# First attention with scores from split halves, and softplus of dt on GpSimd

## The chip, the cores and the metric

The kernel runs on one core of one Trainium2 chip. The metric is the device time of one execution in microseconds (us). A program of this size is compared by the median of several executions.

## The reference, cut to what matters

The program is two blocks of a network over 256 tokens of width 1024, in fp32: an even layer, an odd layer and a further block, each a mixer with projections, attention, and a wide feed-forward. The change lies in the mixer of the even layer, the first stage of the program:

```python
proj = rms_norm(x, mix_norm) @ w_in
q, k, v, z, xbc, dt_raw = jnp.split(proj, EVEN_SPLITS, axis=-1)
q = rms_norm(q.reshape(Bsz, S, 8, 64), na_q_norm)
k = rms_norm(k.reshape(Bsz, S, 8, 64), na_k_norm)
na_out = neighbourhood_attention(q, k, v, na_rel_bias)
...
xbc = jax.nn.silu(centred_depthwise_conv(xbc, conv_w, conv_b))
...
dt = jax.nn.softplus(dt_raw.reshape(Bsz, S, 2, 16) + dt_bias)
A = -jnp.exp(A_log)
y_fwd = ssd_scan(xs, dt[:, :, 0], A[0], bm, cm)
y_bwd = jnp.flip(ssd_scan(jnp.flip(xs, 1), jnp.flip(dt[:, :, 1], 1), A[1], ...), 1)
...
return jnp.concatenate([na_out, ssd_out], axis=-1) @ w_out
```

The attention has 8 heads of 64: its scores are q k^T / 8 plus a bias, over the 256 keys, then a softmax and the values. The scan works in two chunks of 128 tokens; its decays are exponentials of running sums of `dt * A`, so nearly all of it needs dt.

## The kernel before, in words

**Number format.** A product in fp32 takes TensorE two passes. The kernel avoids that for its weights: each fp32 operand is written as a sum of a high part, rounded to the format fp32r, and a low part, the remainder, also in fp32r. A product is then three fp32r matmuls, high by high, high by low and low by high (`mm3`, L144 to L148; they are recorded at L137). For a weight, `wsplit` (L115) has ScalarE copy the loaded block into `wh` (L124) and VectorE subtract it from the block into `wl` (L126); six such pairs of buffers rotate. For activations the same is done behind a transpose.

**Order.** The program is written with generators: `gemm` yields after each block of 128 rows of a weight, `weave` and `pipeline` run several generators in turn, `defer(n, fn)` calls `fn` after n further blocks. The framework under it then schedules the instructions of each engine in an order of its own, by priorities: `tc.high_priority()` lifts what is inside, `pin` keeps an instruction in program order on its engine. So an edit can move instructions far from it. Each engine works through its own queue in order; an instruction that waits holds all behind it. PSUM has eight banks: four for accumulators, two for transposes (`tp_tile`) and two for scores and other short products (`sc_tile`).

**The even mixer up to the scan.** The projections come in the order: q (`e0`), a part of the convolution input, k (`e1`), the rest of the convolution input for the states B and C, then the columns of v and dt (`ev0`), the rest of v (`ev1`). What matters for the change:

- `done_v` (L571) writes the raw dt into `dv` (128 tokens x 64: two halves of the tokens, two directions, 16 heads).
- `softplus` (L220 to L239) computes dt from it. `nv` (L227) is -|v|, ScalarE takes the exponential (L228), `e + 2` (L229) and its reciprocal (L230) give z = e / (e + 2), and the logarithm is a polynomial in z squared (L231 to L236, seven of the steps fused as add and multiply); L237 and L238 add the positive part. All but the exponential is on VectorE, 128 x 64 each, and each step needs the one before. The tiles show as `sp_dt` in the profile. It is called under high priority (L645). The same function serves the forget gate of the last block (L1147).
- `av` (L652) is dt times A. `sums` (L659) multiplies it by triangles on TensorE (`rows`), writes the sums as high and low parts (`LH`, L666 and L667) and sends them through HBM into `RH`. `borders` (L680) makes four further sums (`cps`, L683), their exponentials and `wde` (L685, L686).
- `cb_products` (L599) makes the scan's products of C and B into a bank of `sc_tile`; VectorE takes two masked pieces, `cu` and `cl` (L608), ScalarE the third, `cbo` (L610).
- `qk_T` (L581) transposes q and k into a `tp_tile`; ScalarE copies them, times the norm's gain, into `qkT`, in fp32.
- `na_unit` (L693) is one unit of the attention: two heads by 128 queries. Its scores are two fp32 matmuls of 64 rows by 256 columns (L704). `attn_unit` (L334) adds the bias and takes the minimum on VectorE (L358), the exponential on ScalarE (L366), transposes the result (L141) and multiplies by the values. Eight units run as a pipeline, with the rest of the convolution input (`xbc`, L518 to L520) and the first half of z woven between them.
- `ssd_unit` (L761) is one unit of the scan: the decay sums (`seg`, L774) from `LH` and `RH`, the masked products times dt (`dw`, L778 and L780), minimum, exponential, two weighted copies on GpSimd (`xe`, `xD`), and the products `yp` and `op` (L807, L809). Eight units run in two halves, the first with the last quarter of the convolution, the second with the second half of z and the first products of the output projection `eo`. `gate` and `gate2` take y times z, the norm, and transpose the result for `eo` (`tp_y`, L248).

GpSimd does little before the change: norms' factors, and the scaling of q and k by them (L566).

## Time and profile before

| what | us |
|---|---|
| three runs | 989.68, 989.52, 989.49 |
| their median | 989.52 |
| the profiled execution's own time | 988.49 |
| its span on the core | 986.6 |
| TensorE busy | 968.6 |
| VectorE busy | 652.4 |
| ScalarE busy | 558.8 |
| GpSimd busy | 89.4 |

The granted TensorE clock was 0.999 of full speed over the span. In the lines of the profile, PE is TensorE, PEld its weight loads (beside the matmuls), DVE is VectorE, ACT is ScalarE, POOL is GpSimd and SP the engine that issues most DMAs. L704 is line 704 of the kernel. A line of a timeline has the start in us, the duration, the engine, the line, the operation, the tile written, the tiles read, the size and how many alike follow one another (x4); in square brackets stands what it waited for. A line of windows has a stretch A:B with its length, then for each engine the busy time and the number of instructions, then the granted clock, the busy share of the DMA engines and GB/s. A matmul in fp32 is recorded as two.

### The profile page before, as it was taken

What the parts mean: (1) busy time and instruction counts of PE and PEld (TensorE: products, weight loads), DVE (VectorE), ACT (ScalarE), POOL (GpSimd) and SP (SyncE); (2) the same over time, 40 slices, a digit from 0 to 9 for tenths busy, and PEclk for the clock granted to TensorE, in tenths of its full rate; (3) what the DMA queues carried; (4) which work ended last, traced back from release to release, by engine and by line L of the source; (5) the groups of instructions that cost most, each with busy time, mean ns of one, the idle gap of its engine ahead of it and who ended that gap; (6) DMA issues with size and microseconds to landing.
All of it is one profiled execution on the core that took longest, in us unless ns stands there. A gap on an engine that the chain in (4) does not pass through costs nothing.

```text
span 986.6 us, 13200 instructions
## 1 busy us (share of the span) xinstructions
PE 968.6 (98%) x4983; PEld 809.0 (82%) x4983; DVE 652.4 (66%) x1069; ACT 558.8 (57%) x940; POOL 89.4 (9%) x158
## 2 busy tenths in 40 slices
PE   9999999999999999989999999999999999999998
PEld 7997887788888887788788888889888888888876
DVE  5997789866666455874666666447365966665555
ACT  7775877754445345775555454345676844544442
POOL 1410102110000005320100000001000300000000
PEclk9999999999999999999999999999999999999999
DMA  9664123655555554421265555547423655555541
GB/s 356 232 223 157 64 91 121 214 182 200 172 186 198 187 174 151 171 86 44 88 222 200 174 178 185 207 149 279 166 75 111 233 212 184 200 172 165 190 156 43
DMA packets 29016, 167.69 MB, mean 170 GB/s; under 512 B 3065, under 2 KB 6137, under 8 KB 10777
## 3 DMA queue, kind: packets, MB, share of 16 engines
q1 hardware_dynamic: 28952, 166.85, 48.9%
q8 instruction: 39, 0.64, 0.3%
q14 instruction: 25, 0.20, 0.1%
HBM read 165.72 MB, written 1.11 MB: 169 GB/s over the span
## 4 chain that ended last, share of the span: by engine, by line
PE 89%; DVE 6%; ACT 2%; POOL 1%; issue 1%; DMA 0%; DVEq 0%; ACTq 0%; POOLq 0%
PE acc_fau L137 12%; PE acc_fcu L137 12%; PE acc_fbu L137 12%; PE acc_odd L137 6%; PE acc_mpd L137 6%; PE acc_fd L137 6%; PE so L137 2%; PE acc_e L137 2%; PE acc_pg L137 2%; PE oo L137 2%; PE eo L137 2%; PE acc_z L137 2%; PE xbc L518 2%; PE xbc L519 1%; PE xbc L520 1%; PE o_ga L137 1%
## 5 line engine op out<-in xcount | busy, mean ns | idle before, releaser
L126 DVE TENSOR_TENSOR wl_fau<-raw_fau,wh_fau 128x1024 fp32r<-128x1024 f32 x44 | 53.8, 1223 | 36.7 <-ACT wh_fau L124 36.7
L126 DVE TENSOR_TENSOR wl_fbu<-raw_fbu,wh_fbu 128x1024 fp32r<-128x1024 f32 x44 | 53.7, 1223 | 33.9 <-ACT wh_fbu L124 33.8
L126 DVE TENSOR_TENSOR wl_fcu<-raw_fcu,wh_fcu 128x1024 fp32r<-128x1024 f32 x44 | 53.7, 1222 | 30.3 <-ACT wh_fcu L124 30.2
L137 PE MATMUL acc_fau<-wh_fau,xTl_f 128*128 128x512 f32 x176 | 70.6, 401 | 0.0
L137 PE MATMUL acc_fbu<-wh_fbu,xTl_f 128*128 128x512 f32 x176 | 70.1, 399 | 0.0
L137 PE MATMUL acc_fcu<-wh_fcu,xTl_f 128*128 128x512 f32 x176 | 70.1, 399 | 0.0
L137 PE MATMUL acc_fbu<-wl_fbu,xTh_f 128*128 128x512 f32 x176 | 69.0, 392 | 0.1
L137 PE MATMUL acc_fbu<-wh_fbu,xTh_f 128*128 128x512 f32 x176 | 69.0, 392 | 0.0
L137 PE MATMUL acc_fau<-wl_fau,xTh_f 128*128 128x512 f32 x176 | 68.8, 391 | 0.0
L137 PE MATMUL acc_fcu<-wl_fcu,xTh_f 128*128 128x512 f32 x176 | 68.8, 392 | 0.0
L137 PE MATMUL acc_fau<-wh_fau,xTh_f 128*128 128x512 f32 x176 | 68.7, 390 | 0.0
L137 PE MATMUL acc_fcu<-wh_fcu,xTh_f 128*128 128x512 f32 x176 | 68.7, 390 | 0.0
L124 ACT CAST wh_fau<-raw_fau 128x1024 fp32r<-128x1024 f32 x44 | 46.2, 1049 | 37.1 <-PE acc_fau L137 34.0
L124 ACT CAST wh_fbu<-raw_fbu 128x1024 fp32r<-128x1024 f32 x44 | 46.1, 1050 | 33.3 <-PE acc_fbu L137 31.3
L124 ACT CAST wh_fcu<-raw_fcu 128x1024 fp32r<-128x1024 f32 x44 | 46.3, 1053 | 30.4 <-PE acc_fcu L137 30.3
L126 DVE TENSOR_TENSOR wl_fd<-raw_fd,wh_fd 128x1024 fp32r<-128x1024 f32 x22 | 26.9, 1225 | 26.8 <-ACT wh_fd L124 26.8
L126 DVE TENSOR_TENSOR wl_odd<-raw_odd,wh_odd 128x1024 fp32r<-128x1024 f32 x22 | 26.9, 1225 | 25.8 <-ACT wh_odd L124 25.8
L126 DVE TENSOR_TENSOR wl_mpd<-raw_mpd,wh_mpd 128x1024 fp32r<-128x1024 f32 x22 | 26.9, 1225 | 25.7 <-ACT wh_mpd L124 25.7
L124 ACT CAST wh_fd<-raw_fd 128x1024 fp32r<-128x1024 f32 x22 | 23.0, 1047 | 28.9 <-PE acc_fd L137 23.5
L124 ACT CAST wh_odd<-raw_odd 128x1024 fp32r<-128x1024 f32 x22 | 23.1, 1048 | 28.6 <-PE acc_odd L137 23.2
L124 ACT CAST wh_mpd<-raw_mpd 128x1024 fp32r<-128x1024 f32 x22 | 23.1, 1048 | 28.6 <-PE acc_mpd L137 23.2
L137 PEld LDWEIGHTS acc_fbu<-wl_fbu,xTh_f 128*128 128x128 f32 x176 | 33.0, 188 | 7.4 <-DVE wl_fbu L126 0.6
(519 smaller groups left out, 2813.7 us busy)
## 6 DMA issues: line engine op xcount, KB each, us to landing
raw_fau<-in_w_dram SPq DMA_DIRECT2D x22, 1024.0 KB, 5.0
raw_fbu<-in_w_dram SPq DMA_DIRECT2D x22, 1024.0 KB, 5.2
raw_fcu<-in_w_gu_dram SPq DMA_DIRECT2D x22, 1024.0 KB, 5.0
raw_odd<-in_w_dram SPq DMA_DIRECT2D x10, 1024.0 KB, 4.9
raw_mpd<-in_w_dram SPq DMA_DIRECT2D x10, 1024.0 KB, 4.9
raw_fd<-in_w_dn_dram SPq DMA_DIRECT2D x10, 1024.0 KB, 4.9
raw_xbc<-in_w_xbc_dram SPq DMA_DIRECT2D x8, 1024.0 KB, 5.4
raw_eo<-in_w_out_e_dram SPq DMA_DIRECT2D x6, 1024.0 KB, 5.0
```

What stands on the lines that cost most here:

```text
L124: wsplit.last = act.copy(wh, raw).ins
L126: vec.tensor_tensor(out=wl, in0=raw, in1=wh.bitcast(F32), op=ALU.subtract)
L137: r = pe.matmul(*args, **kw)
L518: pe.matmul(d, lhsT=wh[:, cs], rhs=h0[:, k, :], start=k == 0, stop=False)
L519: pe.matmul(d, lhsT=wh[:, cs], rhs=l0[:, k, :], start=False, stop=False)
L520: pe.matmul(d, lhsT=wl[:, cs], rhs=h0[:, k, :], start=False, stop=k == KD - 1)
```

## The change

It does two things.

**Scores.** `qkT` is now written in fp32r, and for each of the four transposes VectorE makes the low part from PSUM, the transposed values times the gain minus the high part (`qkl`, 128 x 512 each). The low parts of q use the tiles `mBh0` and `mBh1`, those of k one tile `mBl`; these names belong to the scan's output, which is written later. A unit's two fp32 matmuls become six in fp32r, by `mm3`.

**Softplus.** `softplus` has a parameter for the engine. For dt it is GpSimd: the first step (-|v|) and the reciprocal stay on VectorE, the exponential on ScalarE. GpSimd has no fused step here, so each fused one becomes an operation with a scalar and one with two tensors: 23 operations in place of 14. The forget gate stays as it was.

```diff
@@ -217,7 +217,16 @@
         j = sm.tile([P, 512], mybir.dt.bfloat16, tag="junk", name=f"junk_{nm}", bufs=1)
         act.activation(j[:, 0:src.shape[-1]], src, AF.Square, accum_out=acc_ap)
 
-    def softplus(v, n, nm):
+    def softplus(v, n, nm, eng=None):
+
+        eng = vec if eng is None else eng
+
+        def stt(out, in0, scalar, in1, op0, op1):
+            if eng is vec:
+                vec.scalar_tensor_tensor(out=out, in0=in0, scalar=scalar, in1=in1, op0=op0, op1=op1)
+                return
+            eng.tensor_scalar(out=out, in0=in0, scalar1=scalar, scalar2=None, op0=op0)
+            eng.tensor_tensor(out=out, in0=out, in1=in1, op=op1)
 
         nv = sm.tile([P, n], F32, tag="sp0", name=f"sp0_{nm}", bufs=1)
         e = sm.tile([P, n], F32, tag="sp1", name=f"sp1_{nm}", bufs=1)
@@ -226,16 +235,16 @@
         z2 = sm.tile([P, n], F32, tag="sp4", name=f"sp4_{nm}", bufs=1)
         vec.scalar_tensor_tensor(out=nv, in0=v, scalar=-1.0, in1=v, op0=ALU.mult, op1=ALU.min)
         act.activation(e, nv, AF.Exp)
-        vec.tensor_scalar(out=z, in0=e, scalar1=2.0, scalar2=None, op0=ALU.add)
+        eng.tensor_scalar(out=z, in0=e, scalar1=2.0, scalar2=None, op0=ALU.add)
         vec.reciprocal(out=z, in_=z)
-        vec.tensor_tensor(out=z, in0=z, in1=e, op=ALU.mult)
-        vec.tensor_tensor(out=z2, in0=z, in1=z, op=ALU.mult)
-        vec.tensor_scalar(out=q, in0=z2, scalar1=1.0 / 17.0, scalar2=None, op0=ALU.mult)
+        eng.tensor_tensor(out=z, in0=z, in1=e, op=ALU.mult)
+        eng.tensor_tensor(out=z2, in0=z, in1=z, op=ALU.mult)
+        eng.tensor_scalar(out=q, in0=z2, scalar1=1.0 / 17.0, scalar2=None, op0=ALU.mult)
         for d in (15, 13, 11, 9, 7, 5, 3):
-            vec.scalar_tensor_tensor(out=q, in0=q, scalar=1.0 / d, in1=z2, op0=ALU.add, op1=ALU.mult)
-        vec.scalar_tensor_tensor(out=q, in0=q, scalar=1.0, in1=z, op0=ALU.add, op1=ALU.mult)
-        vec.tensor_scalar(out=z2, in0=v, scalar1=0.0, scalar2=None, op0=ALU.max)
-        vec.scalar_tensor_tensor(out=q, in0=q, scalar=2.0, in1=z2, op0=ALU.mult, op1=ALU.add)
+            stt(out=q, in0=q, scalar=1.0 / d, in1=z2, op0=ALU.add, op1=ALU.mult)
+        stt(out=q, in0=q, scalar=1.0, in1=z, op0=ALU.add, op1=ALU.mult)
+        eng.tensor_scalar(out=z2, in0=v, scalar1=0.0, scalar2=None, op0=ALU.max)
+        stt(out=q, in0=q, scalar=2.0, in1=z2, op0=ALU.mult, op1=ALU.add)
         return q
 
     def part(m, t):
@@ -581,15 +590,23 @@
         def qk_T(c):
             halves = []
             for i in range(2):
-                qt = E.tile([P, 2, T], F32, tag="y2", name=f"qkT{c}_{i}", bufs=4)
+                qt = E.tile([P, 2, T], F32R, tag="y2", name=f"qkT{c}_{i}", bufs=4)
+                if c == 0:
+                    ql = E.tile([P, 2, T], F32R, tag=f"mBh{i}", name=f"qkl{c}_{i}")
+                elif i == 0:
+                    kl2 = E.tile([P, 2, 2, T], F32R, tag="mBl", name=f"qkl{c}")
+                if c == 1:
+                    ql = kl2[:, i]
                 tp = tp_tile(f"tqk{c}_{i}")
                 tv = tp.rearrange("p (j t c) -> p j t c", j=2, t=2)
                 for t in range(NT):
                     for j in range(2):
                         pin(pe.transpose(tv[:, j, t, :], qkv[c][t][:, (2 * i + j) * P:(2 * i + j + 1) * P], ident))
-                act.activation(qt, tp.rearrange("p (j s) -> p j s", j=2), AF.Copy,
-                               scale=gq8 if c == 0 else pcol("na_k", 0))
-                halves.append(qt)
+                g = gq8 if c == 0 else pcol("na_k", 0)
+                act.activation(qt, tp.rearrange("p (j s) -> p j s", j=2), AF.Copy, scale=g)
+                vec.scalar_tensor_tensor(out=ql, in0=tp.rearrange("p (j s) -> p j s", j=2), scalar=g,
+                                         in1=qt.bitcast(F32), op0=ALU.mult, op1=ALU.subtract)
+                halves.append((qt, ql))
             qkT.append(halves)
 
         cu = E.tile([P, NT, 4, P], F32, tag="cb3", name="cu", bufs=3)
@@ -643,7 +660,7 @@
         run(v1g, 1)
 
         with tc.high_priority():
-            dtv = softplus(dv.rearrange("p t d h -> p (t d h)"), NT * 32, "dt")
+            dtv = softplus(dv.rearrange("p t d h -> p (t d h)"), NT * 32, "dt", gp)
         dtv = dtv.rearrange("p (t d h) -> p t d h", t=2, d=2)
         eA = sm.tile([P, 32], F32, tag="eA", name="eA", bufs=1)
         act.activation(eA, brow("A_log"), AF.Exp)
@@ -701,7 +718,7 @@
 
             def qk(h, acc):
                 s = slice(e * 64, (e + 1) * 64)
-                pe.matmul(acc, lhsT=qkT[0][i][s, h, t * P:(t + 1) * P], rhs=qkT[1][i][s, h, :], start=True, stop=True)
+                mm3(acc, [q[s, h, t * P:(t + 1) * P] for q in qkT[0][i]], [k[s, h, :] for k in qkT[1][i]], True, True)
 
             return attn_unit(E, f"na{t}_{pr}", qk, T, bias,
                              lambda h, kt: qkv[2][kt].rearrange("p (j e d) -> p j e d", e=2, d=64)[:, 2 * i + h, e, :],
```

The lines below are the engines' queues as the program gives them, row by row; names end in the number of the tile, and in the new kernel line numbers behind the edits are 9 to 17 higher.

VectorE around `av`, before: the softplus steps (`sp_dt`) stand between the weight parts, and `av` comes behind the weight part `wl_z_4`.

```order
L126 TENSOR_TENSOR wl_z_2_1159<-raw_z_0_1152,wh_z_2_1158 128x1024
L235 SCALAR_TENSOR_TENSOR sp_dt<-sp_dt 128x64
L236 SCALAR_TENSOR_TENSOR sp_dt<-sp_dt 128x64
L237 TENSOR_SCALAR sp_dt<-dv 128x64
L238 SCALAR_TENSOR_TENSOR sp_dt<-sp_dt 128x64
L126 TENSOR_TENSOR wl_z_4_1300<-raw_z_4_1297,wh_z_4_1299 128x1024
L652 SCALAR_TENSOR_TENSOR av<-sp_dt,eA 128x32 x2
L780 SCALAR_TENSOR_TENSOR dw_0_1414<-cl,sp_dt,dw_0_1414 128x128 x4
L608 TENSOR_TENSOR cu<-cb_1_965,cst 128x256
L608 TENSOR_TENSOR cl<-cb_1_965,cst 128x256
L126 TENSOR_TENSOR wl_z_6_1304<-raw_z_4_1297,wh_z_6_1303 128x1024
```

And after, the same place (`qkl` are the low parts of q):

```order
L126 TENSOR_TENSOR wl_xbc_4_990<-raw_xbc_4_987,wh_xbc_4_989 128x1024
L126 TENSOR_TENSOR wl_xbc_6_994<-raw_xbc_4_987,wh_xbc_6_993 128x1024
L669 SCALAR_TENSOR_TENSOR av<-sp_dt,eA 128x32 x2
L607 SCALAR_TENSOR_TENSOR qkl_898<-tqk_0_899,pv,qkT_0_897 128x512
L607 SCALAR_TENSOR_TENSOR qkl_898<-tqk_1_907,pv,qkT_1_906 128x512
L126 TENSOR_TENSOR wl_z_0_1183<-raw_z_0_1180,wh_z_0_1182 128x1024
L126 TENSOR_TENSOR wl_z_2_1187<-raw_z_0_1180,wh_z_2_1186 128x1024
L126 TENSOR_TENSOR wl_z_4_1344<-raw_z_4_1341,wh_z_4_1343 128x1024
L797 SCALAR_TENSOR_TENSOR dw_0_1462<-cl,sp_dt,dw_0_1462 128x128 x4
L625 TENSOR_TENSOR cu<-cb_1_981,cst 128x256
L625 TENSOR_TENSOR cl<-cb_1_981,cst 128x256
L126 TENSOR_TENSOR wl_z_6_1348<-raw_z_4_1341,wh_z_6_1347 128x1024
```

The steps of the softplus have left the queue, and `av` now stands behind `wl_xbc_6`, ahead of `wl_z_0`, `wl_z_2` and `wl_z_4`, which were ahead of it; the two low parts of q stand behind it. GpSimd's queue has the 23 steps in a row behind its last work on k (`qkv`).

TensorE at the first scores (`sc_na_0`), before; `cb` is the last of the scan's four products of C and B:

```order
L604 MATMUL cb_1_1017<-bc_177,bc_175 128x256 x2
L683 MATMUL cps<-av,cst 128x16 x4
L518 MATMUL xbc_0_903<-h_82,wh_xbc_6_977 128x256
L519 MATMUL xbc_0_903<-l_83,wh_xbc_6_977 128x256
L520 MATMUL xbc_0_903<-h_82,wl_xbc_6_978 128x256
L704 MATMUL sc_na_0_1031<-qkT_0_884,qkT_0_695 128x256 x2
L518 MATMUL xbc_1_904<-h_82,wh_xbc_6_977 128x256
L519 MATMUL xbc_1_904<-l_83,wh_xbc_6_977 128x256
L520 MATMUL xbc_1_904<-h_82,wl_xbc_6_978 128x256
```

And after:

```order
L621 MATMUL cb_1_1033<-bc_177,bc_175 128x256 x2
L700 MATMUL cps<-av,cst 128x16 x4
L527 MATMUL xbc_0_919<-h_82,wh_xbc_6_993 128x256
L528 MATMUL xbc_0_919<-l_83,wh_xbc_6_993 128x256
L529 MATMUL xbc_0_919<-h_82,wl_xbc_6_994 128x256
L137 MATMUL sc_na_0_1047<-qkT_0_897,qkT_0_695 128x256
L137 MATMUL sc_na_0_1047<-qkl_898,qkT_0_695 128x256
L137 MATMUL sc_na_0_1047<-qkT_0_897,qkl_0_696 128x256
L137 MATMUL sc_na_0_1047<-qkT_0_897,qkT_0_695 128x256
```

The place is the same. A head's two passes in fp32 (one row of the queue) are three rows.

TensorE at the transposes of the last y (`tp_y_1`) for the output projection, before:

```order
L137 MATMUL eo_0_2024<-wh_eo_6_2100,mBh_0_1584 128x512
L137 MATMUL eo_0_2024<-wl_eo_6_2101,mBh_0_1584 128x512
L137 MATMUL eo_0_2024<-wh_eo_6_2100,mBl_1586 128x512
L137 MATMUL eo_1_2025<-wh_eo_6_2100,mBh_1_1585 128x512
L137 MATMUL eo_1_2025<-wl_eo_6_2101,mBh_1_1585 128x512
L137 MATMUL eo_1_2025<-wh_eo_6_2100,mBl_1586 128x512
L248 MATMUL tp_y_1_1993<-cst,y_1_1942 128x128 x4
L137 MATMUL eo_0_2024<-wh_eo_6_2100,mBh_0_1584 128x512
L137 MATMUL eo_0_2024<-wl_eo_6_2101,mBh_0_1584 128x512
```

And after:

```order
L137 MATMUL eo_0_2072<-wh_eo_2_2080,mAh 128x512
L137 MATMUL eo_0_2072<-wl_eo_2_2081,mAh 128x512
L137 MATMUL eo_0_2072<-wh_eo_2_2080,mAl 128x512
L137 MATMUL eo_1_2073<-wh_eo_2_2080,mAh 128x512
L137 MATMUL eo_1_2073<-wl_eo_2_2081,mAh 128x512
L137 MATMUL eo_1_2073<-wh_eo_2_2080,mAl 128x512
L257 MATMUL tp_y_1_2041<-cst,y_1_1990 128x128 x4
L137 MATMUL eo_0_2021<-wl_eo_4_2111,mBh_0_1632 128x512
L137 MATMUL eo_0_2021<-wh_eo_4_2110,mBl_1634 128x512
L137 MATMUL eo_1_2022<-wl_eo_4_2111,mBh_1_1633 128x512
```

The transposes stand earlier: the products of the output projection ahead of them are now those of its first weight blocks (`eo` from `wh_eo_2` with `mAh`, the attention's output), no longer those of the blocks `wh_eo_4` and `wh_eo_6`. Between the first decay product `seg` and these transposes stand 50 `eo` matmuls where there were 90, and 47 of `xbc` where there were 77; on VectorE 12 weight parts are in that stretch where there were 18. The queue of SP has the same rows in the same order.

## Prediction

> **What bounds the kernel now.** I read the page first (busy shares and the chain that ended last), then the stages by windows, then the timelines of TensorE, VectorE, ScalarE and GpSimd through the stage that the change touches.
>
> ```profile
> PE 968.6 (98%) x4983; PEld 809.0 (82%) x4983; DVE 652.4 (66%) x1069; ACT 558.8 (57%) x940; POOL 89.4 (9%) x158
> ...
> PE 89%; DVE 6%; ACT 2%; POOL 1%; issue 1%; DMA 0%; DVEq 0%; ACTq 0%; POOLq 0%
> ```
>
> TensorE sets the time: 98% busy, 89% of the chain. Two kinds of edit count: one that shortens TensorE's own work, and one that makes TensorE wait. The first mixer has two stages of interest (columns: PE, PEld, DVE, ACT, POOL, clock, DMA):
>
> ```profile
> 80.00:118.00 38.00, 38.00 (x235) 30.64 (x234) 27.56 (x85) 27.18 (x70) 4.80 (x4) 1.00 0.33 103
> 118.00:180.00 62.00, 60.13 (x337) 50.21 (x336) 56.55 (x103) 47.02 (x102) 10.23 (x12) 1.00 0.32 107
> ```
>
> In 80 to 118 us, where the scores stand, TensorE is never idle. In 118 to 180 us VectorE is at 91%, and TensorE already loses 1.87 us.
>
> **Part 1, the scores (TensorE).** Rows around the first scores, and further on:
>
> ```profile
> 75.39 1.05 PE L664 MATMUL rows<-cst,av 128*16 128x128 f32 x8
> ...
> 77.90 1.02 PE L604 MATMUL cb<-bc,bc 128*128 128x256 f32 x4
> 78.77 0.96 PE L683 MATMUL cps<-av,cst 128*128 128x16 f32 x8
> ...
> 79.90 0.28 PE L520 MATMUL xbc<-h,wl_xbc 128*128 128x256 f32 x1
> 80.11 1.13 PE L704 MATMUL sc_na<-qkT,qkT 64*128 64x256 f32 x4
> 81.16 0.38 PE L518 MATMUL xbc<-h,wh_xbc 128*128 128x256 f32 x1
> 81.39 0.28 PE L519 MATMUL xbc<-l,wh_xbc 128*128 128x256 f32 x1
> ```
>
> ```profile
> 102.27 0.70 PE L704 MATMUL sc_na<-qkT,qkT 64*128 64x256 f32 x2
> 102.90 1.10 PE L137 MATMUL o_na<-qkv,pT_na 128*128 128x64 f32 x8
> 103.93 0.70 PE L704 MATMUL sc_na<-qkT,qkT 64*128 64x256 f32 x4
> 104.56 0.66 PE L141 MATMUL pt_na<-cst,p_na 128*128 128x128 f32 x4
> ```
>
> A product in f32 is two records, so a unit (two heads) is x4. Split products of 256 columns start 0.12 us apart. From 79.90 to 81.39 is 1.49 us, which without the scores would be two such steps, 0.24: a unit costs 1.25 us. Five of the eight units stand like this. The other three are spread over four places of 0.63 us (102.27 to 102.90, 103.93 to 104.56, and two more), 2.52 us in all. After the change a unit is 6 split products. Nearest for a split product that uses only part of the array's rows is the decay product:
>
> ```profile
> 164.92 0.39 PE L774 MATMUL seg<-RH,LH 72*128 72x512 f32 x1
> 165.15 0.40 PE L137 MATMUL eo<-wl_eo,mAh 128*128 128x512 f32 x1
> ```
>
> It takes 0.23 us for 512 columns, just as a full one, so I take 0.12 for 256: 0.72 a unit. Gain: 5 x 0.53 + (2.52 - 18 x 0.12 = 0.36) = 3.0 us, all on TensorE. The bound on the other side: if each split product took the 0.265 us of a present record, a unit would be 1.59 us and the eight would lose 2.7 us. The row of 72 partitions is far nearer; I keep 3.0.
>
> **Part 2, the low parts (VectorE).** Four new subtractions of 128x512 out of PSUM. Their like:
>
> ```profile
> L254 DVE TENSOR_TENSOR mAl<-tp_nao,mAh 128x512 fp32r<-128x512 f32 x2 | 1.4, 685 | 0.8 <-ACT mAh L253 0.8
> ```
>
> In a queue, instructions start some 0.08 us sooner than their busy time says (62.76 below: 0.21 busy, 0.13 apart), so 0.60 each, 2.4 in all. Fourteen small ones of 0.13 to 0.23 leave, 2 to 3 us. VectorE's sum is even; the places are not. ScalarE's four copies only change the type they write (nothing). The tiles lent by mBh0, mBh1 and mBl are written again some 25 us after the last score (nothing). SP's queue keeps its order row for row.
>
> **Part 3, softplus on GpSimd, and who waits.** Rows of VectorE and ScalarE now:
>
> ```profile
> 61.63 1.21 DVE L126 TENSOR_TENSOR wl_xbc<-raw_xbc,wh_xbc 128x1024 fp32r<-128x1024 f32 x1
> 62.76 0.21 DVE L227 SCALAR_TENSOR_TENSOR sp_dt<-dv 128x64 f32<-128x64 f32 x1
> 62.89 0.75 DVE L543 SCALAR_TENSOR_TENSOR bc<-cth,cy 128x256 f32<-128x256 f32 x2
> ...
> 64.80 0.54 DVE L230 RECIPROCAL sp_dt<-sp_dt 128x64 f32<-128x64 f32 x1
> 65.27 0.35 DVE L608 TENSOR_TENSOR cu<-cb,cst 128x256 f32<-128x256 f32 x1
> ...
> 73.39 0.29 DVE L652 SCALAR_TENSOR_TENSOR av<-sp_dt,eA 128x32 f32<-128x32 f32 x2
> 73.59 1.14 DVE L780 SCALAR_TENSOR_TENSOR dw<-cl,sp_dt,dw 128x128 f32<-128x128 f32 x4
> 74.64 0.42 DVE L608 TENSOR_TENSOR cu<-cb,cst 128x256 f32<-128x256 f32 x1
> ...
> 75.31 1.22 DVE L126 TENSOR_TENSOR wl_z<-raw_z,wh_z 128x1024 fp32r<-128x1024 f32 x1
> 77.08 0.68 DVE L667 TENSOR_TENSOR LH<-rows,LH 16x512 fp32r<-16x512 f32 x1 [0.56 <-ACT LH L666]
> ```
>
> ```profile
> 63.00 0.26 ACT L228 ACTIVATE sp_dt<-sp_dt 128x64 f32<-128x64 f32 x1 [0.71 <-DVE sp_dt L227]
> ...
> 75.48 0.37 ACT L610 COPY cbo<-cb 128x256 f32<-128x256 f32 x1 [0.83 <-DVE cl L608]
> ```
>
> and what GpSimd takes:
>
> ```profile
> 14.44 0.40 POOL L497 TENSOR_SCALAR cw<-pv 128x64 f32<-128x64 f32 x1 [12.96 <-DMA pv<-in_pvec_dram]
> ...
> 46.90 3.33 POOL L566 TENSOR_TENSOR qkv<-qkv,r_qk 128x512 f32<-128x512 f32 x1
> ...
> 53.17 1.09 POOL L566 TENSOR_TENSOR qkv<-qkv,r_qk 128x512 f32<-128x512 f32 x1
> ...
> 381.68 0.46 POOL L875 TENSOR_TENSOR Cgk<-cst,bv 128x128 f32<-128x128 f32 x1
> ...
> 384.41 0.95 POOL L880 TENSOR_TENSOR Sgk<-cst,bv 128x32 f32<-128x32 f32 x4
> ...
> 385.68 0.19 POOL L212 TENSOR_SCALAR ms_od<-sst_od 128x1 f32<-128x1 f32 x1
> 385.95 0.57 POOL L213 TENSOR_TENSOR r_od<-ms_od,mhalf 128x1 f32<-128x1 f32 x1
> ```
>
> ```profile
> 47.23 2.09 DVE L126 TENSOR_TENSOR wl_ev<-raw_ev,wh_ev 128x576 fp32r<-128x576 f32 x3
> 49.51 1.80 DVE L126 TENSOR_TENSOR wl_ev<-raw_ev,wh_ev 128x1024 fp32r<-128x1024 f32 x1 [0.18 <-ACT wh_ev L124]
> ```
>
> Start: ahead of nv (62.76) VectorE now has two subtractions (1.2) and one pair bc (0.67) more and one weight part (1.13) less, so nv starts at 63.5; one weight part follows, then the reciprocal, which waits for exp and GpSimd's first step: 65.3 to 65.8. GpSimd goes on at 65.9.
>
> Length: 22 instructions are left, 11 with a scalar and 11 with two tensors (each fused one became two). One with a scalar takes 0.40. One with two tensors lies between 0.24 (128x32) and 0.46 (128x128): 0.33. Each needs the one before, which adds 0.08 (385.68 + 0.19 to 385.95). 11 x (0.48 + 0.41) = 9.8 us.
>
> Contention: at 46.90 a step of 1.09 us took 3.33 while weight parts ran without a gap, and the weight part at 49.51 took 1.80 instead of 1.21. GpSimd stood still until that row of parts was over. In the new order wl_xbc_4 and wl_xbc_6 fall into the softplus, 2.3 us. So it ends at T = 65.9 + 9.8 + 2.3 = 78.0; without that, 75.3 (the first step also comes sooner).
> The Trainium skill, "SBUF — State Buffer", section "Who interferes with whom", says that a VectorE instruction with two SBUF inputs and a GpSimd instruction that reads SBUF lock each other out for the whole instruction. The two rows agree; by its rule T is the later of the two.
>
> Behind it: in the new order the first VectorE instruction that needs the result, av, stands right behind wl_xbc_6, which ends at 69.4. VectorE is blocked from there to T, and all that is queued behind av comes after T: 0.3 for the hand-over and av, two subtractions 1.2, three weight parts wl_z 3.39, four dw 1.05, cu and cl 0.67 (74.64 to 75.31): T + 6.6. The copy cbo and its hand-over, 0.5, free the PSUM bank: T + 7.1. TensorE needs that bank for the product cb that now runs at 77.90. The next weight part (1.13) and LH (0.60) end at T + 8.35 and free the bank for cps, now at 78.77. The first score stands 1.34 us behind cps, now 80.11, then T + 9.8. Where TensorE waits: first at rows (75.39) for av, then at cb for some 4.3 us, and a little at cps. Late in all: T + 9.8 - 80.1 = 7.7 us with T = 78.0, 5.0 with 75.3. I take 7.7. From the first score on VectorE and TensorE stand to each other as now, so nothing gives it back: TensorE has no idle time left to 118 us.
>
> **Part 4, the moved order.** Between the first decay product and the last y transposes TensorE has 30 split products of 256 columns and 40 of 512 less (0.12 and 0.23: 12.8 us), so 60.1 becomes 47.3 us; VectorE has 18 weight parts before and 12 after, 6.8 us less, so 56.6 becomes 49.8. VectorE is then the longer one. At a full queue TensorE idles 2.5 us instead of 1.9; at today's 91% the stage is 54.6 us and it idles 7.3. So +0.6 to +5.4; if waits vanished, -1.9. I take +2, near the full queue, since it is the order of the two queues that was changed.
>
> **Sum.** The profiled execution took 988.49 us (span 986.6 and 1.9 around it); the median of the three runs is 989.52, 1.03 above. -3.0 + 7.7 + 2.0 = +6.7: 995.2 for such an execution, 996.2 as a median.
>
> **Rivals.** About 0.2% (2 us) is what a measurement here tells from no change.
>
> - *GpSimd is quick, TensorE never waits (faster).* The stall is gone if T + 9.8 is at most 80.1: T = 70.3, 0.2 us an instruction. Then only the 3.0 us remain: 986.5. It begins to win at T = 73.3, 0.34 an instruction. Against it: 0.40 at 14.44 for this very shape. For it: the new order has av so early. Chance 0.11. The Trainium skill, "GPSIMD Engine Reference", section "Elementwise — side-by-side cycle accounting", gives 2.6 cycles an element at 1.2 GHz and 4497 ns for 2048 elements, which makes about 0.2 us for 64, an estimate, and T = 70.3; the row at 14.44 says twice that.
> - *It cancels (no change).* No contention (5.0 us late), the scores' 3.0, and stage 118 to 180 loses its waits (-1.9): +0.1, 989.6; or T near 73.3. Chance 0.11.
> - *Much slower.* Stage 118 to 180 stays at 91% (+5.4), and after 4.3 us of idleness TensorE comes back at half its clock: cb to the first score, 2.2 us (77.90 to 80.11), take twice that. -3.0 + 7.7 + 5.4 + 2.2 = +12.3: 1001.8. For it: 91% is what the stage does now; against: the granted clock is 1.00 throughout, but no such gap stands in this trace. Chance 0.10. The Trainium skill, "TensorE: Matmul & The Clock Gate", section "What's actually happening", has the clock halve after an idle window of about 3.4 us; no run here shows it yet.
>
> **How the numbers follow.** The forecast (996.2) has 0.68. The range goes from the cancelled case, 989.5, to the much slower one, 1002; outside are the quick GpSimd and the ends beyond. Faster 0.11 is the first rival; no change 0.13 is the second and the forecast's lower edge; slower 0.76 is the rest.
>
> **What would show it.** Right: GpSimd's 23 steps span some 12 us, with a gap while two weight parts run; av starts near 78 instead of 73.4 and VectorE is idle before it by 8 us, released by GpSimd; TensorE idles before rows, cb and cps; the first score starts near 88; scores 0.12 apart. Wrong: av before 73, or no gap of TensorE before 80 us.

## The result, and the profile after

The changed kernel takes 1013.02 us (median of five, 1012.61 to 1015.24), the one before 989.68 (five, 989.49 to 989.83): a ratio of 1.0245, with an interval of 1.0234 to 1.0256. The forecast was 996.2, with a range of 989.5 to 1002.0: the sign was right, the size was not. The loss is 23.3 us, and 6.7 were forecast.

From the page of the changed kernel:

```profile
PE 983.8 (97%) x4999; PEld 823.5 (81%) x4999; DVE 651.6 (64%) x1059; ACT 559.5 (55%) x940; POOL 100.9 (10%) x181
...
PEclk9996898999999999999999999999999999999999
...
PE 88%; DVE 5%; POOL 3%; ACT 2%; issue 1%; DVEq 0%; POOLq 0%; ACTq 0%
```

The shares read as before, and TensorE is even busier, by 15 us. That is no more work: in the row of the clock, three of the 40 slices (about 25 us each) are clearly below full speed. The stages by windows, with the columns of the prediction:

```profile
82.00:107.00 25.00, 22.66 (x77) 18.60 (x78) 15.33 (x45) 10.12 (x25) 0.00 (x0) 0.52 0.46 137
107.00:164.00 57.00, 54.73 (x364) 47.87 (x364) 41.46 (x104) 40.96 (x95) 5.80 (x7) 1.00 0.17 58
164.00:172.00 8.00, 4.96 (x14) 3.58 (x15) 3.45 (x6) 4.27 (x13) 7.66 (x6) 0.57 0.71 262
172.00:188.00 16.00, 13.61 (x75) 11.39 (x73) 15.43 (x32) 13.70 (x29) 1.24 (x2) 1.00 0.01 2
188.00:192.00 4.00, 3.84 (x12) 3.13 (x13) 3.12 (x6) 2.31 (x9) 0.00 (x0) 0.57 0.64 193
```

The granted clock is at half in three stretches of this stage, and TensorE idles for some 8 us between 107 and 192. GpSimd, VectorE, ScalarE and TensorE around the first stretch:

```profile
67.09 0.38 POOL L242 TENSOR_SCALAR sp_dt<-sp_dt 128x64 f32<-128x64 f32 x1
67.55 1.31 POOL L228 TENSOR_SCALAR sp_dt<-sp_dt 128x64 f32<-128x64 f32 x1
68.94 1.04 POOL L229 TENSOR_TENSOR sp_dt<-sp_dt 128x64 f32<-128x64 f32 x1
...
76.75 0.32 POOL L229 TENSOR_TENSOR sp_dt<-sp_dt 128x64 f32<-128x64 f32 x1
```

```profile
67.41 2.39 DVE L126 TENSOR_TENSOR wl_xbc<-raw_xbc,wh_xbc 128x1024 fp32r<-128x1024 f32 x2
77.10 0.29 DVE L669 SCALAR_TENSOR_TENSOR av<-sp_dt,eA 128x32 f32<-128x32 f32 x2 [7.30 <-POOL sp_dt L229]
77.31 1.40 DVE L607 SCALAR_TENSOR_TENSOR qkl<-tqk,pv,qkT 128x512 fp32r<-128x512 f32 x2
78.63 3.49 DVE L126 TENSOR_TENSOR wl_z<-raw_z,wh_z 128x1024 fp32r<-128x1024 f32 x3
82.03 1.13 DVE L797 SCALAR_TENSOR_TENSOR dw<-cl,sp_dt,dw 128x128 f32<-128x128 f32 x4
```

```profile
83.92 0.37 ACT L627 COPY cbo<-cb 128x256 f32<-128x256 f32 x1 [3.65 <-DVE cl L625]
```

```profile
79.77 0.28 PE L529 MATMUL xbc<-h,wl_xbc 128*128 128x256 f32 x1
84.34 2.08 PE L621 MATMUL cb<-bc,bc 128*128 128x256 f32 x4 [4.29 <-ACT cbo L627]
...
88.70 0.58 PE L137 MATMUL sc_na<-qkT,qkT 64*128 64x256 f32 x1
89.08 0.41 PE L137 MATMUL sc_na<-qkl,qkT 64*128 64x256 f32 x1
```

This is the stall of the prediction, link by link: GpSimd's chain with two steps held while two weight parts run, av behind it, VectorE's queue behind av, cbo, and TensorE's gap of 4.29 us (4.3 forecast). What was not forecast stands in the last two rows: the cb that took 1.02 us takes 2.08, and split products start 0.21 us apart instead of 0.12. The clock halved during the gap, at 82.6, and came back only at 106.5.

The later stage: TensorE's waits from 125 to 215 us, before (us in total, times, longest) and after:

```profile
PE yp L807 <- DVE m L788: 1.1, 1, 1.1
PE txs L548 <- DVE xsT L543: 0.5, 1, 0.5
PE seg L774 <- DVE m L786: 0.2, 1, 0.2
```

```profile
PE tp_y L257 <- ACT y L757: 5.4, 3, 2.4
PE acc_z L137 <- DVE wl_z L126: 1.2, 1, 1.2
PE txs L557 <- DVE xsT L552: 0.7, 1, 0.7
PE yp L824 <- DVE m L805: 0.6, 1, 0.6
```

and how the longest wait for y comes about, in the changed kernel:

```profile
163.34 1.22 DVE L126 TENSOR_TENSOR wl_z<-raw_z,wh_z 128x1024 fp32r<-128x1024 f32 x1
164.48 2.36 DVE L126 TENSOR_TENSOR wl_eo<-raw_eo,wh_eo 128x1024 fp32r<-128x1024 f32 x2
```

```profile
163.74 3.15 POOL L212 TENSOR_SCALAR ms_g<-s 128x2 f32<-128x2 f32 x1 [11.06 <-ACT junk_g L218]
```

```profile
167.69 0.91 ACT L757 ACTIVATE y<-y,r_g 128x256 f32<-128x256 f32 x2 [3.08 <-POOL r_g L213]
```

```profile
168.26 0.69 PE L257 MATMUL tp_y<-cst,y 128*128 128x128 f32 x2 [2.42 <-ACT y L757]
```

TensorE comes to the transposes of y with little work of its own left ahead of them. The norm's factor, a step of two elements on GpSimd, takes 3.15 us, as long as three weight parts run on VectorE; the other three of its kind take 0.19 to 0.54 here, and 0.19 to 0.34 in the kernel before. And the clock is at half again, from 164.5 to 171.3. It had fallen ahead of this wait, behind two shorter ones:

```profile
162.96 0.44 PE L557 MATMUL txs<-cst,xsT 128*128 128x128 f32 x2 [0.70 <-DVE xsT L552]
164.62 0.79 PE L137 MATMUL acc_z<-wl_z,h 128*128 128x512 f32 x1 [1.22 <-DVE wl_z L126]
```

### The profile page after: what moved, and what is told of

The parts are those of the page before. It is cut to its first block, busy times and chain, and to the rows that moved or that the text cites. A ratio compares the mean times of both kernels' runs of the same rounds, so it can differ in the third digit from the quotient of the medians.

```text
span 1013.1 us, 13239 instructions
## 1 busy us (share of the span) xinstructions
PE 983.8 (97%) x4999; PEld 823.5 (81%) x4999; DVE 651.6 (64%) x1059; ACT 559.5 (55%) x940; POOL 100.9 (10%) x181
## 4 chain that ended last, share of the span: by engine, by line
PE 88%; DVE 5%; POOL 3%; ACT 2%; issue 1%; DVEq 0%; POOLq 0%; ACTq 0%
PE acc_fau L137 12%; PE acc_fcu L137 12%; PE acc_fbu L137 12%; PE acc_mpd L137 6%; PE acc_odd L137 6%; PE acc_fd L137 6%; PE eo L137 3%; PE acc_e L137 2%; PE so L137 2%; PE acc_pg L137 2%; PE oo L137 2%; PE acc_z L137 2%; PE xbc L527 1%; PE xbc L528 1%; PE o_ga L137 1%; PE xbc L529 1%
## 5 line engine op out<-in xcount | busy, mean ns | idle before, releaser
L527 PE MATMUL xbc<-h,wh_xbc 128*128 128x256 f32 x128 | 38.7, 304 | 0.9 <-ACT qkv L582 0.9
```

Source lines behind the costliest of these rows:

```text
L527: pe.matmul(d, lhsT=wh[:, cs], rhs=h0[:, k, :], start=k == 0, stop=False)
```

## The experiments

The theory after the result: the loss has three parts. A: TensorE waits for the softplus. B: the gap throws the clock to half, far beyond the stage's start. C: the order of the later stage, which both edits together bring about, costs by itself. Rivals: the scores themselves lower the clock, and the later stage suffers only because it starts late. The kernel before took 989.3 to 989.8 beside these runs.

### The two edits apart

**Scores alone.** `softplus(..., "dt", gp)` goes back to `softplus(..., "dt")`.

> Scores split as in the change, softplus of dt back on VectorE. Theory A (a gap of TensorE behind the GpSimd softplus, then a clock at half for some 22 us): without the softplus there is no gap over 1 us ahead of the first score, the granted clock is 1.00 from 60 to 118 us, and the scores bring their 3.0 us: 986.5, give or take 2 for the order in the later stage, which moves another way here. Rival B (the split products of 64 rows themselves lower the clock): the clock is 0.5 from the first score on for some 18 us, 9 us lost: 995 or more.

Measured: 989.47 against 989.31, ratio 1.0009 (0.9999 to 1.0018): no change. The clock is 1.00 from 40 to 240 us and no gap over 1 us stands ahead of the scores, so the scores don't lower it. But they don't bring 3.0 us either. One unit between full products:

```profile
84.29 0.28 PE L529 MATMUL xbc<-h,wl_xbc 128*128 128x256 f32 x1
84.50 0.38 PE L137 MATMUL sc_na<-qkT,qkT 64*128 64x256 f32 x1
84.72 0.28 PE L137 MATMUL sc_na<-qkl,qkT 64*128 64x256 f32 x1
...
85.20 0.28 PE L137 MATMUL sc_na<-qkT,qkl 64*128 64x256 f32 x1
85.40 0.50 PE L137 MATMUL acc_z<-wh_z,h 128*128 128x512 f32 x1
85.74 0.40 PE L137 MATMUL acc_z<-wl_z,h 128*128 128x512 f32 x1
```

From 84.29 to 85.74 is 1.45; without the scores it would be 0.12 + 0.23, so a unit costs 1.10, not 0.72. The products are 0.12 apart, as forecast; the other 0.38 lie where TensorE goes from 128 rows to 64 and back (0.21 instead of 0.12 into the first, 0.22 behind it, 0.20 out, 0.34 instead of 0.23 behind that). The last block of z is 0.9 us earlier than before (145.0 for 145.9); then a wait of 1.9 for y, which the kernel before doesn't have, takes that back.

**Softplus alone.** The scores stay in fp32 with two passes.

> Softplus of dt on GpSimd, scores in fp32 as before; TensorE's order is that of before, row for row. Theory A: VectorE comes to cu and cl 1.3 us sooner than in the change, since two subtractions less stand behind av, so TensorE's gap ahead of cb is about 3.0 us. If that is short enough for the clock, the first score is some 5 us late and the total 994 to 995; if the clock falls as it did after 2.6 us of idleness, 10 us more, 1004 to 1006. In both cases no wait over 1 us for the last y, since the order there is that of before. Rival B (the clock fell for the split scores): no half clock, 995 whatever the gap. Rival C (the later stage suffers from the softplus itself): waits for y appear here too.

Measured: 1000.38, ratio 1.0120 (1.0105 to 1.0135). The gap ahead of cb is 2.97 us, and the clock is at half from 83 to 100, with the scores of before: the fall belongs to the gap. The first score comes at 85.6. No wait for y appears, so the softplus alone doesn't bring part C.

### The gap and the clock

**The gap filled.** Ahead of the last cb on TensorE, into a bank that nobody reads:

```diff
+            if (s, gp2) == (1, 1):
+                fill = tp_tile("fill")
+                for _ in range(18):
+                    pin(pe.matmul(fill, lhsT=h0[:, 0, 0:P], rhs=h0[:, 0:2, :].rearrange("p k t -> p (k t)"),
+                                  start=True, stop=True))
```

> The change, with 18 products of 512 columns that nobody reads put ahead of the last cb on TensorE, 4.1 us of work in its 4.3 us gap; the order of the rest moves by a few rows only. Theory A: the clock stays at 1.00 through the stall, so the 21.9 us at half clock (84.34 to 106.2) take 10.9 less: about 1002, with the first score at 86.5 rather than 88.7. Rival B (the scores lower the clock): half clock from the first score on, 1010 to 1013.

Measured: 1005.53, 7.5 less than the change. Its windows:

```profile
80.00:107.00 27.00, 26.56 (x139) 20.89 (x137) 22.21 (x54) 13.88 (x30) 0.00 (x0) 1.00 0.58 178
```

The delay is still there (first score at 86.8, 6.7 later than before), the half clock is not. Work added to TensorE made the kernel 7.5 us faster; that is part B. 10.9 were expected. From first score to feed-forward the filled kernel needs 123.1 us; the change, less the 8.9 that its half clock costs behind the first score, needs 120.8: a later stage that follows a slow TensorE waits less. That the other engines had got ahead meanwhile is argued, not shown.

**A shorter softplus.** `for d in (15, 13, 11, 9, 7, 5, 3)` becomes `(7, 5, 3)` for dt.

> The change with four of the seven polynomial steps of the dt softplus left out (8 GpSimd instructions fewer; the logarithm is then less exact). Theory A: GpSimd ends 8 x 0.43 = 3.4 us sooner, the gap ahead of cb shrinks from 4.3 to about 1 us, the clock does not fall: 3.4 + 10.9 = 14 us less, 999. If the loss were only the delay (no part of the clock): 3.4 less, 1009.6.

Measured: 1005.42, in four runs of 1001.28, 1005.40, 1005.45 and 1009.38. The gain is larger than the delay alone would give (1009.6) and smaller than the full theory's (999): cb starts 3.7 us sooner (80.66), but TensorE also ran out of work sooner, the gap is still 2.2, and the clock falls for three windows of 3.41 us (82.8 to 93.0).

**How long the half clock lasts.** Worked out from the granted clock in windows of 1 us, the half clock lasted 23.9, 6.8 and 3.4 us in the change, 17.1 with the softplus alone, 10.2, 6.8 and 3.4 with the shorter one: 7, 2, 1, 5, 3, 2 and 1 times 3.41. The Trainium skill, "TensorE: Matmul & The Clock Gate", section "What's actually happening", gives a free-running window of 4096 cycles at 1.2 GHz, 3413 ns, and says that one busy window brings the clock back. The lengths agree; one busy window does not: TensorE was busy without a gap from 84.34, and five windows passed before the one that counted. These five hold 0.7 (with cps beside them), 1.3, 1.3, 1.7 and 1.7 us of scores, the one that counted none. To see whether the scores' 64 rows are the reason, all rows of both tiles were used:

```diff
-                s = slice(e * 64, (e + 1) * 64)
+                s = slice(0, P)
```

> The change, with each score product over all 128 rows of the two tiles instead of the 64 of its head (the scores are then sums over two heads); every queue has the same rows in the same order. So far the half clock lasted whole windows of 3.41 us: seven in the change, five with the softplus alone, three with the shorter softplus, and each window that failed to bring the clock back held 1.2 us or more of scores, the one that did 0.8 or less. Theory A1 (products of 64 rows count too little as activity): with 128 rows the window with cps still fails and the next passes, so the clock is back near 92.9 instead of 106.5, four windows less, 6.8 us; the changes between 64 and 128 rows, 0.38 a unit, go too: 1003 to 1006. Theory A2 (the length has nothing to do with the rows): still seven windows, 1010 or more.

Measured: 1005.32. Its windows:

```profile
84.00:92.00 8.00, 7.96 (x38) 7.29 (x39) 4.06 (x11) 2.77 (x8) 0.00 (x0) 0.57 0.60 192
92.00:107.00 15.00, 15.00 (x85) 12.88 (x84) 13.71 (x35) 10.04 (x21) 0.00 (x0) 1.00 0.50 152
```

Two windows instead of seven, with the same gap of 4.3 us and the same queues: products over 64 rows keep the clock down once it is down. At full clock they don't bring it down (scores alone). The windows lie elsewhere in this execution (the fall comes at 84.6, not at 82.6), but all four executions are between 1005.0 and 1005.8 us and all five of the change between 1012.6 and 1015.2, so one lucky place does not explain it.

**av off VectorE.** GpSimd makes av at the end of its chain, and nothing else moves.

```diff
-            vec.scalar_tensor_tensor(out=av[:, t], in0=dtv[:, t], scalar=-1.0,
-                                     in1=eA.rearrange("p (d h) -> p d h", d=2), op0=ALU.mult, op1=ALU.mult)
+            gp.tensor_tensor(out=av[:, t], in0=dtv[:, t], in1=eA.rearrange("p (d h) -> p d h", d=2), op=ALU.mult)
```

with `eA` negated beforehand.

> The change, with av made by GpSimd at the end of the softplus, so that VectorE is not held at av; all other rows stay in place. Theory L (VectorE's subtractions hold GpSimd): two qkl, wl_z_0 and wl_z_2 now run during the softplus and hold it 3 to 4 us, so it ends near 80.5 instead of 77.1; wl_z_4 still waits for its high part, which stands behind dw on ScalarE, and cb comes at the end of the softplus + 5.3, 86 instead of 84.3: 1013 to 1017, nothing won. Rival (no such hold): the softplus ends at 77.1, cb at 82.4, the gap is 2.3 instead of 4.3 us: 1007 to 1011.

Measured: 1007.26, in runs of 1004.62 to 1012.34; the median lies in the rival's range, but by luck, since the steps are not the rival's. VectorE and GpSimd:

```profile
69.80 1.41 DVE L607 SCALAR_TENSOR_TENSOR qkl<-tqk,pv,qkT 128x512 fp32r<-128x512 f32 x2
71.13 2.48 DVE L126 TENSOR_TENSOR wl_z<-raw_z,wh_z 128x1024 fp32r<-128x1024 f32 x2
```

```profile
70.87 0.37 POOL L228 TENSOR_SCALAR sp_dt<-sp_dt 128x64 f32<-128x64 f32 x1
71.32 1.20 POOL L229 TENSOR_TENSOR sp_dt<-sp_dt 128x64 f32<-128x64 f32 x1
72.61 1.22 POOL L228 TENSOR_SCALAR sp_dt<-sp_dt 128x64 f32<-128x64 f32 x1
73.92 0.32 POOL L229 TENSOR_TENSOR sp_dt<-sp_dt 128x64 f32<-128x64 f32 x1
```

The weight parts (both inputs in SBUF) hold GpSimd, each step for one part; the low parts qkl (one input from PSUM) do not. The Trainium skill's rule of the prediction ("SBUF — State Buffer", "Who interferes with whom") speaks of two SBUF inputs, and this agrees. The chain ends at 78.75 (80.5 by Theory L, 77.1 by the rival), and cb starts at 84.18, nearly as in the change (84.34), since the third weight part waits 7.1 us for its high part on ScalarE, as Theory L had it. But TensorE's wait is now in two pieces, 2.7 us at rows and 1.0 at cb, and in the profiled execution the clock fell for one window (3.4 us) instead of seven.

Whether a gap near this size brings the clock down also depends on something else than the gap. Two waits in the odd layer, which no edit touches, the first in the kernel before and in the changed one, the second in the kernel before (us in total, times, longest):

```profile
394.24 0.66 PE L936 MATMUL tk<-cst,kd 128*128 128x128 f32 x4 [1.88 <-ACT kd L930]
```

```profile
419.30 0.66 PE L953 MATMUL tk<-cst,kd 128*128 128x128 f32 x4 [1.88 <-ACT kd L947]
```

```profile
PE pt_ga L141 <- DVE qS L966: 2.5, 1, 2.5
```

The same 1.88 us leave the clock full in the one and cost a window at half from 420.5 to 423.9 in the other. The changed kernel has the wait of 2.5 us too, and in both it leaves the clock full. In the kernel with the last steps on GpSimd (below) the same two waits cost a window each, at 394.9 and 432.4.

The traces show what else counts. In each trace all changes of the clock lie on one grid of 3.41 us: in the changed kernel the falls at 164.5, 188.4 and 420.5 are 24, 31 and 99 windows behind the one at 82.6. So the windows run on by themselves, whatever the kernel does. In eight traces the clock fell, 24 times from 40 us on. Cut along the grid of its trace, the window ahead of each fall has TensorE busy for 0.8 to 1.6 us, but for one with 1.86 (the shorter softplus, with the small products cps in it). Of the windows at full clock that no fall followed, the least busy had 1.73. In these runs, then, the clock falls behind a window that is busy for less than about half, and a gap of 2 us makes such a window or not by how the grid cuts it.

The clock also accounts for the runs of one kernel that lie 4 us and more apart. With the shorter softplus the mean granted clock of the four executions was 0.992, 0.988, 0.988 and 0.984, fastest first, and 0.004 of some 1005 us is the 4.0 us between them; with av on GpSimd it was 0.991 at 1004.62 us and 0.984 at 1012.34. It bears on small differences too. Beside these runs the kernel before was executed 62 times, 14 times at a mean clock of 0.999 (987.6 to 988.5 us) and 48 times at 0.996 to 0.998 (989.2 to 990.9). A window at half clock is worth 1.7 us, so those 48 look like executions with such a window; that is argued, since its one trace is of an execution at 0.999.

### The later stage

**One step on GpSimd.** Scores split; of the softplus only `e + 2` on GpSimd (`eng = vec` behind the reciprocal). The order of TensorE's queue is that of the change, row for row.

> Scores split as in the change, and of the dt softplus only the first step (e + 2) on GpSimd, the rest back on VectorE. TensorE's queue is then that of the change, row for row, while VectorE's steps stand between its weight parts as before, so av comes in time. Theory O (the order of the later stage, which both edits together bring about, is a loss of its own): no gap and no half clock to 118 us, but the same waits for y (some 5.8 us in all) and the same windows at half clock (two and one) in the later stage, where the kernel with the filled gap lost 9.9 us between first score and feed-forward: 999 to 1001. Rival (the later stage suffers only because it starts late, behind the stall): no such waits, 989 to 991.

Measured: 999.44, ratio 1.0109 (1.0096 to 1.0122). The clock is full to 148 us, the first score comes at 80.7, and the waits from 125 to 215 us are:

```profile
PE tp_y L258 <- ACT y L758: 5.4, 3, 2.5
PE acc_z L137 <- DVE wl_z L126: 1.2, 1, 1.2
```

The longest two are shown; they are the change's, and so are the two falls of the clock (148.8 to 155.7 and 172.7 to 176.2), without any stall ahead of them. Part C is a loss of its own: 10.0 us, or 10.9 with the 0.9 of the scores in it. All waits of this stretch come to 7.9 us where the kernel before has 1.8.

**The last steps on GpSimd.** `eng` is set to GpSimd only from the maximum with zero on (L237 of the kernel before); the later order is then near that of before.

> Scores split as in the change, and of the dt softplus only the last three GpSimd instructions on GpSimd. The later stage's order is then that of before to within a few rows (90 products of the output projection ahead of the last y instead of 50 in the change). If order alone decides the later stage: its waits are those of before, the scores keep the 0.9 us that they gained alone, 988.5 to 989; if VectorE's four new subtractions or a late av take it back: 989.5 to 991.

Measured: 989.82, ratio 1.0008 (1.0000 to 1.0017). The waits for y are down to 0.5 us, so with both kinds of edit in the program part C is gone when the order is. The scores' 0.9 are still not in the time (988.9 to 989.3 in the six executions at a clock of 0.999, where the kernel before takes 987.6 to 988.5); why not stays open.

**The other gaps filled too.** To the filled kernel, 12 and 8 such products ahead of the transposes of the second and third y (`keep["h"]` is `h0`).

```diff
+        for _ in range({"y0_1": 12, "y1_0": 8}.get(nm, 0)):
+            pin(pe.matmul(tp, lhsT=keep["h"][:, 0, 0:P], rhs=keep["h"][:, 0:2, :].rearrange("p k t -> p (k t)"),
+                          start=True, stop=True))
```

> The kernel with the filled gap, and 12 and 8 more products that nobody reads put ahead of the transposes of the second and the third y, where TensorE waited 2.9 and 2.0 us and the clock then fell for two windows and one. If these falls of the clock come from those waits: no half clock any more, 3.4 + 1.7 = 5.1 us less, about 1000.5. If they come from something else in that stage, half clock stays and the fill costs up to 4.5: 1005 to 1010.

Measured: 1004.16, only 1.4 less than the filled kernel, though the clock is full from 40 to 240 us. The falls do come from the waits there, but here they cost little: waits for the decays of 2.0 us appear in their place, and the fill itself takes 20 x 0.23 = 4.6. In this stage TensorE waits for the chain of y, so what a faster TensorE gains it waits away.

**Scores alone, gate later.** `defer(2, ...)` of `gate2` becomes `defer(4, ...)`.

> Scores alone, and the last step of the gate put off by two more blocks, which moves the transposes of y against the other work. Scores alone gained 0.9 us by its stage's end and lost it again in waits for y (1.9) and for the decays. If the order is what takes it back: without the wait for y 987.5 to 988.5; if every order has its own waits there: 989 to 991.

Measured: 990.22, ratio 1.0012 (1.0004 to 1.0021). The wait for y stays (2.0), and one for the decays grows to 1.9. Another order brought other waits.

### The scores

**Scores alone over 128 rows.** The edit of the 128 rows above, on the scores alone.

> Scores alone, each score product over all 128 rows of its tiles instead of the 64 of its head (the scores are sums over two heads); all queues as with the scores alone. A unit of six split products cost 1.10 us there, 0.72 of it start to start and 0.38 around it, where TensorE changes from 128 rows to 64 and back. If those changes are what the forecast's 3.0 us left out: a unit takes 0.72 here, 8 x 0.38 = 3.0 us less on TensorE, and if the later stage takes no more than it took from the scores alone, 986.5; if it takes back whatever the scores win, 989. If the 0.38 stay, the rows are not their cause.

Measured: 986.81, ratio 0.9972 (0.9961 to 0.9983). A unit now starts its six products 0.12 apart with 0.12 on either side (0.72 in all). The last block of z starts at 143.2, 2.7 us earlier than before: nearly all of the forecast's 3.0 us were there but for the changes of rows. At the start of the feed-forward 1.5 of them are left (191.8 for 193.3). The medians differ by more, 2.8, and part of that is the clock: all seven executions here had a mean clock of 0.999 or more, of the 15 of the kernel before only two.

**Pairs of heads.** Scores alone, the products of the two heads of a tile issued in turn, and `run(xg, 6)` becomes `run(xg, 7)`:

```diff
+                for h in range(2):
+                    for n, (a, b) in enumerate(((0, 0), (0, 1), (1, 0))):
+                        for ee in range(2):
+                            s = slice(ee * 64, (ee + 1) * 64)
+                            pin(pe.matmul(svs[ee][:, h, :], lhsT=qkT[0][i][a][s, h, t * P:(t + 1) * P],
+                                          rhs=qkT[1][i][b][s, h, :], start=n == 0, stop=n == 2))
```

> Scores alone, with the two units of a tile (heads in rows 0 to 63 and in rows 64 to 127) issued together, product by product in turn, into both banks, and the first unit one block of the convolution later, which brings the later stage's order near that of before. A version that could beat both. If two products in different rows run beside each other: 4 pairs of 0.38 + 6 x 0.12 = 1.1 us in place of 8 x 1.10, 4.4 us less: 985 to 986. If they run one after the other but with half the changes of rows: 4 x 0.38 = 1.5 less: 988. If the later stage or the wait for the banks takes it back: 989 to 991.

Measured: 987.29, ratio 0.9983 (0.9973 to 0.9993), 0.2% faster than the kernel before; the feed-forward starts 2.0 us earlier (191.3 for 193.3). One pair:

```profile
94.91 0.39 PE L733 MATMUL sc_na<-qkT,qkT 64*128 64x256 f32 x2
95.14 0.28 PE L733 MATMUL sc_na<-qkl,qkT 64*128 64x256 f32 x2
...
95.60 0.28 PE L733 MATMUL sc_na<-qkT,qkl 64*128 64x256 f32 x2
95.81 0.44 PE L141 MATMUL pt_na<-cst,p_na 128*128 128x128 f32 x2
```

Two products in different halves of the rows run beside each other: twelve take the 0.90 us that six took. The Trainium skill, "TensorE: Matmul & The Clock Gate", section "The mechanism", says so of products in different row groups. Of the 4.4 us expected, 2.4 arrive in the medians (1.7 by the ratio); waits for y (1.5) and for the decays (0.7) are still there.

## Why the prediction was wrong, step by step

**TensorE bounds the kernel, and the stall: right.** GpSimd's steps took 0.37 and 0.32 (0.40 and 0.33 forecast), the hold 1.7 us (2.3), and T was 77.1 (78.0). The order of releases behind it held to the end. Without the clock the stall cost 6.1 us (filled kernel 1005.53 against 999.44 with one step), where 7.7 stood in the sum. That the first score came near 88, as its signs had it, was in part luck: T + 9.8 with the measured T is 86.9, where the filled kernel has it (86.8), and the half clock under cb and cps brought it to 88.7.

**The clock: a step that failed.** The prediction named the half clock as part of a rival with a chance of 0.10 and priced it over "cb to the first score, 2.2 us (77.90 to 80.11)"; in the sum it had no term. It ended the price where its own chain ended, and never asked what brings the clock back. The runs showed 24 us at half clock, 7.5 us of time. Every trace with a gap of about 3 us or more at cb (2.97, 4.29 and 4.29) shows the fall, so this was the likely case and not one of ten. The trace of before, with 2.5 us at full clock, could not show that.

**The moved order: the other step that failed.** "+2 (−1.9 to +5.4)" came from VectorE's busy sum against TensorE's. Measured: 10.9. The fewer products ahead of the transposes were read as less work for TensorE, not as less cover for the chain of y (norm on GpSimd, scaling on ScalarE, transposes on TensorE). In the prediction's own terms, 40 products of 0.23 us fewer, 9.2 us of cover gone, and a norm step that can be held like the softplus: both were in view, and the waits that they make were not worked out. The waits grew by 6.1 us (7.9 against 1.8), a little more than the upper end of its range; the half clock in this stage, 10.2 us long, had no price in it. The two don't simply add, as the filling of these gaps showed. So even the "much slower" rival, which named both causes, came to no more than 1001.8.

**The scores: the mechanism right, a term mis-sized.** The old unit's 1.25 us held the changes of rows, and the new unit's 0.72 left them out; the row that was taken as nearest, the decay product of 72 rows, shows no such cost. 0.9 us were won, not 3.0, and the later stage takes even those back. The "two passes" of a product in fp32 are two records in the trace, each of about 0.26 us from start to start (80.11 to 81.16 for four) where a split product takes 0.12; so much of the forecast held. Two side sums are wrong as well, though nothing in the forecast hangs on them. The bound on the other side is eight units of 1.59 us against 8.77 now (5 x 1.25 + 2.52), 4.0 us lost and not 2.7. And the first rival's estimate of about 0.2 us comes to 0.14 an instruction by the two figures of the Trainium skill that stand beside it, 0.22 with the 0.08 between steps; 0.37 and 0.32 were measured.

**The sum.** Forecast: −3.0 + 7.7 + 2.0 = +6.7. By the runs: −0.9 + 6.1 (stall) + 7.5 (clock behind it) + 10.9 (order, with its own half clock) = +23.6; 23.3 were measured. That these agree is no proof: the terms are differences along one chain of kernels (before, one step, filled, the change), so they must come to the whole but for the spread of the medians. What shows each cause is the run that takes it away alone.

## What to carry to other kernels

Where an edit opens a gap of some 2 us or more on TensorE, ask whether it leaves a window of 3.41 us less than half busy, and price the half clock to the point where full products run for a whole window, not to the end of the gap. Where a scheduler moves a consumer ahead of work that stood before it, count that work as the cover of the consumer's producer, even if its own engines are not full. And ask of a short run of small products what it costs to change to them and back. Before a difference of a microsecond is put down to an edit, compare the mean granted clocks of the executions.

## What the runs showed of the hardware

- Gaps of 2.2, 3.0 and 4.3 us halved TensorE's clock in three kernels, for whole windows of 3.41 us; one of 1.88 us and one of 2.5 us did so in some kernels and not in others.
- In one trace all changes of the clock lie on one grid of 3.41 us; each of 24 falls followed a window of it with TensorE busy for 0.8 to 1.9 us, and no window with less than 1.73 left the clock full.
- Products over 64 rows let the clock stay at half: seven windows with them, two when the products ran over 128 rows.
- Going to 64 rows and back costs 0.38 us a unit, and two products in different halves of the rows run at the same time: twelve products of 256 columns in 0.90 us.
- VectorE's subtraction with both inputs in SBUF holds a GpSimd step for the length of a weight part (1.20 instead of 0.32); one with an input from PSUM doesn't (0.37).
